# Memory's products moved behind the first group's queries, with x's rows and query weights loaded ahead of memory, and two row tiles begun with products of high parts

## The chip, the cores and the metric

The kernel runs on 1 core of one Trainium2 chip. The metric is device time in microseconds of one execution; the median of several runs is compared. The engines are TensorE (PE, matmuls, with its weight loads shown as PEld), VectorE (DVE), ScalarE (ACT), GpSimd (POOL) and SyncE (SP), which here only issues DMA transfers from its queue (SPq).

## The reference

An encoder trunk of two layers on 512 tokens of width 1024, in fp32. Each layer mixes tokens, then applies a gated feed-forward net, with RMS norms before and after each. What matters here is the start of the first layer, whose mixer is banded attention (12 query heads in 3 groups, 3 key and value heads) beside 4 heads of attention on a memory of 256 rows:

```python
mem_n = rms_norm(mem, mem_norm_g)
for i in range(DEPTH):
    h = rms_norm(x, g_mix_pre[i])
    proj = h @ w_in[i]                 # q | k | v | qm
    ...                                # kind 0: rotary on part of q and k, banded attention with a sink per head
    mkv = mem_n @ w_mem_kv[i]          # km | vm, 256 rows
    mo = memory_attention(qm, km, vm)
    o = jnp.concatenate([tok, mo], axis=-1) @ w_o[i]
    x = x + rms_norm(o, g_mix_post[i])
    h = rms_norm(x, g_ffn_pre[i])
    gu = h @ w_gate_up[i]
    f = (jax.nn.silu(gu[..., :D_FF]) * gu[..., D_FF:]) @ w_down[i]
    x = x + rms_norm(f, g_ffn_post[i])
```

## The kernel before

Precision: every fp32 operand is split into a high part (a rounded copy, fp32r) and a low part (the rest). A product is three matmuls (`mm3`, lines 276 to 278): high by high, high by the weights' low part (`wlo`), low by the weights' high part (`whi`). The high part is made by ScalarE (line 286, or 303 with a gain) or GpSimd (284, 301), the low part by VectorE (290, 304) or GpSimd (288). A unit's `side` says who: bit 2 puts the high part on GpSimd, bit 1 the low part.

Tiles: x is 4 row tiles of 128 tokens, its width 8 column tiles of 128 (`KD`). Transposed copies of x and of memory come from the host (`xT`, `memT`); `hT` and `mT` are their high and low parts with the norm's gain, while each row's own factor (`rs`, `rm`) is worked out from the plain rows (`row`, `mh`) and applied to the product. Weights come in units of two or four column tiles (`unit`): a raw buffer (`raw`, 3 of them) is loaded, then split into `whi` and `wlo` (4 buffers of each), mostly in two halves. All four units of the key and value weights (`wkv`) sit in those 4 buffers until tile 3 has used them; the next four units take them over in the order in which they were asked for.

Order on TensorE is written out by hand in `mixer`: `put(x, f)` lays a step at a coordinate x, and the steps are issued in the order of x. Head h of the attention begins at x = h; `kstep`, `q0step` and other entries of the table `PACE` give the length of a step. For layer 0 the start is, in this order: key and value products of the 4 row tiles (`kv_pieces`, each of 4 steps u of two column tiles, the first two tiles interleaved by the table `FIRST`), the transposes of their keys (`keys`), the products of the first group of queries (`q_pieces` with c = 0, 4 row tiles of 4 steps), the products of memory's keys and values (`mem_pieces`: 4 steps u for 2 row tiles m of memory), the first steps of query group 1, and the scores of head 0 (`score`, line 574). Memory's steps u = 0 and 1 stand right behind the last key product and ahead of the first query product; u = 2 and 3 lie between steps of the queries:

```python
xm = [max(xq + pc["m0off"], xk + 3.8 * k if l else xk)]
xm.append(xm[0] + pc["m0dur"])
```

The other engines' and SP's instructions are ordered by a planner with costs of its own, which follows the order in which the program asks for them where data and buffers allow; only the loads in `loads` are chained to go out one behind the other. `LATE` gives the coordinates of the work that is made on demand: forms of x's tiles 2 and 3, row factors `("r", t)`, memory's forms `("m", m)`, memory's plain rows (`"rows"`) and factors `("rm", m)`. Behind memory's last step `tok` copies `mT` (2 MB) to DRAM for layer 1, and the attention's output then takes its place. In `start`, 14 matmuls on zeros run while the first loads are on their way.

Of the kernel before, what the change touches and what calls it, by code (L numbers as in the profile page):

```python
# [16 lines left out]
P = 128  # L17
# [15 lines left out]
BIG = 1e37  # L33
NFILL = 3
URGENT = 150
FIRST = ((0, 0.25, 1, 1.5), (0.5, 0.75, 1.25, 1.75))
LATE = {2: 1.2, ("r", 0): 1.05, ("r", 1): 1.3, 3: 2.2, ("r", 2): 2.4, ("m", 0): 2.8, ("m", 1): 3.2, ("r", 3): 3.4,
        "rows": 2.5, ("rm", 0): 4.4, ("rm", 1): 4.5}
LOTS = ((0, 8), (8, 14), (14, 22))

PACE = [{'lag': 1.692, 'vlag': 0.479, 'jstep': 0.213, 'kstep': 0.375, 'klag': 0.742, 'qoff': [0.212, 0.126, 0.099], 'qlag': 1.02, 'late': 0.6, 'moff': -0.235, 'mdur': 0.562, 'mlag': 0.697, 'kw': [0, 0, 2, 0], 'mw': [2, 1, 1, 0], 'qw': [1, 0, 0, 1, 3, 3, 3, 3], 'hoff': 0, 'ow': [10.3, 10.8, 12.2, 13.2], 'ox': 11.4, 'od': 0.3, 'hstep': 0.872, 'hlag': 1.742, 'hjstep': 0.135, 'hvlag': 0.751, 'owm': [0, 0, 0, 0, 0, 0, 0, 0], 'q0step': 0.27, 'q0off': -0.032, 'q0lag': 0.919, 'm0off': -0.078, 'm0dur': 0.002, 'm0lead': 1.887, 'mlead': 1.201, 'qlead': 0.921, 'q0lead': 1.555, 'qstep': 1.002, 'tw': [0, 0, 0, 0, 0, 0, 0, 0], 'h2off': 0}, {'lag': 1.824, 'vlag': 0.535, 'jstep': 0.218, 'kstep': 0.777, 'klag': 1.715, 'qoff': [-0.027, -0.162, -0.027], 'qlag': 1.189, 'late': 2.15, 'moff': -0.088, 'mdur': 0.384, 'mlag': 1.205, 'kw': [0, 0, 0, 0], 'mw': [0, 0, 0, 0], 'qw': [0, 0, 0, 0, 0, 3, 1, 1], 'hoff': 0, 'ow': [10.2, 10.7, 12.2, 13.2], 'ox': 11.3, 'od': 0.3, 'hstep': 0.946, 'hlag': 1.847, 'hjstep': 0.295, 'hvlag': 0.568, 'owm': [0, 0, 0, 0, 0, 0, 0, 0], 'q0step': 0.718, 'q0off': -0.018, 'q0lag': 1.136, 'm0off': -1.059, 'm0dur': 0.171, 'm0lead': 2.465, 'mlead': 3.162, 'qlead': 1.895, 'q0lead': 1.42, 'qstep': 0.998, 'tw': [0, 0, 0, 0, 0, 0, 0, 0], 'h2off': 0.016}]

# [143 lines left out]
class Trunk:  # L186
# [195 lines left out]
    def mem_pieces(self, l, mk, put, x0, dx, lag, xw):  # L382

        nc = self.nc
        w, ps = {}, []
        for u in range(4):
            self.unit(self.a["wm"][l, u], self.side(l, "mw", u), put=put, x=xw[u], dst=w, key=u,
                      early=("wm", u) if l == 0 else None)

        def prod(u, m):  # L390
            if u == 0:
                ps.append(self.tagged("s"))
            for k in (2 * u, 2 * u + 1):
# [73 lines left out]
    def kv_pieces(self, l):  # L467
        nc = self.nc
        self.ka = self.core.tile([P, NG, S], F32R, name="ka", tag="ka")
        self.kb = self.core.tile([P, NG, S], F32R, name="kb", tag="kb")  # L470
        self.vs = self.core.tile([P, NT, NG, P], F32R, name="vs", tag="vs")
        w = self.wkv

        def prod(t, st, u):
            self.ready(t)
            if u == 0:
                st["ps"] = self.tagged("acc" if t < 2 else "s")
            ps = st["ps"]
            for k in (2 * u, 2 * u + 1):
                c = slice((k % 2) * 384, (k % 2) * 384 + 384)  # L480
                self.mm3(ps[:, :384], self.hslice(0, k, t * P, t * P + P), self.hslice(1, k, t * P, t * P + P),
                         w[u][0][:, c], w[u][1][:, c], k == 0, k == KD - 1)
            if u == 3:
                self.ready(("r", t))
                kv = ps[:, :384].rearrange("p (z h d) -> p z h d", z=2, d=HD)
                r = self.rs[:, t:t + 1]
                kx = self.core.tile([P, 4, HD], F32, tag="qx", name="kx", bufs=3)
                ins = nc.scalar.activation(kx[:, :NG], kv[:, 0], AF.Copy, scale=r).ins
                self.split_scaled(self.vs[:, t, :, :HD], self.vs[:, t, :, HD:], kv[:, 1], r)
                if l:  # L490
                    with self.tc.issue_after(ins):
                        z, ks = t // 2, slice(t % 2 * 4, t % 2 * 4 + 4)
                        nc.sync.dma_start(self.mT[:, z, ks].bitcast(F32), self.spill[:, z, ks])
                r = self.rope(l, kx, t, NG, 1)
                if l:
                    nc.vector.tensor_mul(kx[:, :NG], kx[:, :NG], r[:, :NG, None].to_broadcast([P, NG, HD]))
                st["k2"] = self.core.tile([P, 4, 3 * HD], F32R, tag="q2", name="k2", bufs=3)
                self.split(st["k2"][:, :NG, :HD], st["k2"][:, :NG, HD:P], kx[:, :NG])
                self.again(st["k2"][:, :NG])

        out = []
        for t in range(NT):
            st = {}
            out.append(([lambda t=t, st=st, u=u: prod(t, st, u) for u in range(4)],
                        lambda t=t, st=st: self.keys(st["k2"], self.ka, self.kb, t, NG)))
        return out

# [167 lines left out]
    def mixer(self, l, mkp, late, tokp):  # L675
# [59 lines left out]
        for z, key in enumerate(list(late)):  # L735
# [2 lines left out]
        lay(self.kv_pieces(l), xk, k, pc["klag"], lambda t: 0 if l else max(0, t - 1) / 4, None if l else FIRST)  # L738
        lay(self.q_pieces(l, 0, qT, put, xq + pc["q0off"], pc["q0lead"]), xq + pc["q0off"], pc["q0step"], pc["q0lag"],
            lambda t: t / 4)  # L740
        xm = [max(xq + pc["m0off"], xk + 3.8 * k if l else xk)]
        xm.append(xm[0] + pc["m0dur"])
        xm.append(max(xm[1] + pc["m0dur"], pc["moff"] - 1))
        xm.append(xm[2] + pc["mdur"])
# [405 lines left out]
    def start(self, mkp):  # L1150
# [3 lines left out]
        with ExitStack() as st:  # L1154
# [49 lines left out]
        def row(t):  # L1204
            rows[t] = [self.core.tile([P, 512], F32, tag=z, name="row", bufs=4) for z in ("th", "tl")]
            for z in range(2):
                queued(rows[t][z], a["x"][0, t * P:(t + 1) * P, 512 * z:512 * z + 512])

        def turn(t):
            xT.append(turned("xT"))  # L1210
            for z in range(2):
                queued(xT[t][:, 4 * z:4 * z + 4], a["xT"][t, z])

        def mem_turn(m):
            mT.append(turned("memT"))
# [145 lines left out]
```

## Time and profile before

| | us |
|---|---|
| median of 3 runs (1116.82 to 1117.99) | 1117.63 |
| profiled execution | 1118.46 |
| its span | 1116.6 |
| TensorE busy in the span | 1091.1 |
| VectorE busy | 842.1 |
| ScalarE busy | 660.1 |
| GpSimd busy | 196.7 |

The span is the time from the first to the last instruction of the profiled execution; its own time is 1.86 us longer. Busy times of engines overlap. A profile names an instruction by line, engine and operation, with what it writes and reads (`ps<-whi,mT`: a matmul into `ps` from those two tiles), and an idle time by what ended it. The granted clock is TensorE's, 1.00 at full speed. The start of the first layer up to the first score ends at 63.53 us.

### The profile page before, as it was taken

To read this page: it belongs to the slowest core of one execution; us is meant where nothing else is said; L and a number is where in the kernel's file an instruction comes from. 1 tells how busy PE (TensorE), PEld (TensorE's weight loads), DVE (VectorE), ACT (ScalarE), POOL (GpSimd) and SP (SyncE) were. 2 spreads that over 40 slices of the span, in tenths; PEclk is the share of its full clock that TensorE was granted. 3 is DMA by queue.
4 is the path that set the end of the run, shared out by engine and by line. 5 is a ranking of instruction groups with operands and counts; after the bars stand their busy time and mean duration, and the time that the engine had idled before them with its cause. 6 is when DMAs were issued, how large, how long until landed. Compare 5 with 4: busy or idle time off the path is not lost.

```text
span 1116.6 us, 19512 instructions
## 1 busy us (share of the span) xinstructions
PE 1091.1 (98%) x7438; PEld 1002.4 (90%) x7438; DVE 842.1 (75%) x1430; ACT 660.1 (59%) x1359; POOL 196.7 (18%) x340
## 2 busy tenths in 40 slices
PE   8899999999999999999999999999999999999997
PEld 7799988999889989998898888878999899899986
DVE  6778886899547867885787988767996478669855
ACT  6678984766445634653467788756664255345631
POOL 4574331202000000000343453312000000000001
PEclk9999999999999999999999999999999999999999
DMA  8621016443753372325443221145136223412253
GB/s 314 227 77 49 28 38 227 151 151 116 244 181 112 113 273 89 97 81 211 163 167 114 76 77 38 38 152 189 39 114 213 70 80 114 148 64 98 87 169 114
DMA packets 40557, 142.43 MB, mean 128 GB/s; under 512 B 4624, under 2 KB 5008, under 8 KB 40336
## 3 DMA queue, kind: packets, MB, share of 16 engines
q1 hardware_dynamic: 40176, 140.66, 36.5%
q8 instruction: 58, 0.95, 0.4%
q10 hardware_dynamic: 288, 0.53, 0.2%
q14 instruction: 35, 0.29, 0.1%
HBM read 122.30 MB, written 18.87 MB: 126 GB/s over the span
## 4 chain that ended last, share of the span: by engine, by line
PE 87%; DVE 6%; ACT 3%; POOL 2%; issue 1%; DMA 1%; DVEq 0%; POOLq 0%; ACTq 0%
PE ps L277 14%; PE ps L278 14%; PE ps L276 14%; PE ps L1034 12%; PE ps L1032 12%; PE ps L1033 12%; PE tp L635 3%; PE o L650 2%; PE o L649 2%; PE s L574 1%; PE s L575 1%; DVE tl L290 1%; DVE wlo L290 1%; DMA pair<-whi 1%; POOL r L310 1%
## 5 line engine op out<-in xcount | busy, mean ns | idle before, releaser
L286 ACT ACTIVATE whi<-raw 128x512 fp32r<-128x512 f32 (+3 forms) x204 | 168.7, 843 | 175.5 <-PE ps L1034 73.7
L290 DVE TENSOR_TENSOR wlo<-raw,whi 128x1024 fp32r<-128x1024 f32 (+3 forms) x199 | 192.5, 980 | 75.7 <-ACT whi L286 72.0
L1033 PE MATMUL ps<-sf,wlo 128*128 128x256 f32 x640 | 179.7, 281 | 0.0
L1032 PE MATMUL ps<-sf,whi 128*128 128x256 f32 x640 | 179.7, 281 | 0.0
L1034 PE MATMUL ps<-sf,whi 128*128 128x256 f32 x640 | 179.7, 281 | 0.0
L277 PE MATMUL ps<-wlo,f 128*128 128x512 f32 (+1 forms) x360 | 138.7, 385 | 0.1
L276 PE MATMUL ps<-whi,f 128*128 128x512 f32 (+1 forms) x360 | 138.7, 385 | 0.0
L278 PE MATMUL ps<-whi,f 128*128 128x512 f32 (+1 forms) x360 | 138.4, 385 | 0.0
L1034 PE MATMUL ps<-a,whi 128*128 128x256 f32 x480 | 134.4, 280 | 0.0
L1032 PE MATMUL ps<-a,whi 128*128 128x256 f32 x480 | 134.3, 280 | 0.0
L1033 PE MATMUL ps<-a,wlo 128*128 128x256 f32 x480 | 133.8, 279 | 0.0
L1033 PEld LDWEIGHTS ps<-sf,wlo 128*128 128x128 f32 x640 | 121.4, 190 | 0.5
L1032 PEld LDWEIGHTS ps<-sf,whi 128*128 128x128 f32 x640 | 121.1, 189 | 0.5
L1034 PEld LDWEIGHTS ps<-sf,whi 128*128 128x128 f32 x640 | 121.4, 190 | 0.0
L319 POOL TENSOR_SCALAR e<-sso 128x1 f32<-128x1 f32 x8 | 3.4, 421 | 564.3 <-ACT junk L314 564.2
L276 PE MATMUL ps<-whi,hT 128*128 128x256 f32 (+1 forms) x320 | 99.0, 309 | 1.3 <-ACT whi L286 1.3
L277 PE MATMUL ps<-wlo,hT 128*128 128x256 f32 (+1 forms) x320 | 94.7, 296 | 2.5 <-DVE wlo L290 2.5
L625 POOL TENSOR_SCALAR p<-p,rd 128x256 f32<-128x256 f32 (+2 forms) x128 | 76.8, 617 | 102.5 <-DVE rd L622 44.9
L278 PE MATMUL ps<-whi,hT 128*128 128x256 f32 (+1 forms) x320 | 94.2, 294 | 0.0
L1033 PEld LDWEIGHTS ps<-a,wlo 128*128 128x128 f32 x480 | 90.5, 188 | 0.2
L1032 PEld LDWEIGHTS ps<-a,whi 128*128 128x128 f32 x480 | 90.4, 188 | 0.2
L1034 PEld LDWEIGHTS ps<-a,whi 128*128 128x128 f32 x480 | 90.1, 188 | 0.0
(203 smaller groups left out, 2697.9 us busy)
## 6 DMA issues: line engine op xcount, KB each, us to landing
raw<-in_wgu_dram SPq DMA_DIRECT2D x48, 512.0 KB, 4.4
raw<-in_wd_dram SPq DMA_DIRECT2D x44, 512.0 KB, 4.4
rb<-in_wgu_dram SPq DMA_DIRECT2D x40, 512.0 KB, 3.6
raw<-in_wo_dram SPq DMA_DIRECT2D x17, 512.0 KB, 4.1
raw<-in_wq_dram SPq DMA_DIRECT2D x16, 512.0 KB, 5.1
xt<-x SPq DMA_DIRECT2D x12, 512.0 KB, 4.8
raw<-in_wm_dram SPq DMA_DIRECT2D x8, 512.0 KB, 4.0
x<-y SPq DMA_DIRECT2D x8, 512.0 KB, 2.9
```

The lines of the kernel that those rows point to most:

```text
L276: mm(out, lh, rh, start=first, stop=False)
L277: mm(out, lh, rl, start=False, stop=False)
L278: mm(out, ll, rh, start=False, stop=last)
L286: a = nc.scalar.activation(hi, src, AF.Copy)
L290: b = nc.vector.tensor_sub(lo, src, hi.bitcast(F32))
L625: self.pooled = nc.gpsimd.tensor_scalar(hd["p"][z][:, :n], hd["p"][z][:, :n], rd[:, z:z + 1], 1.0, op0=OP.mult, op1=OP.mult)
L635: nc.tensor.transpose(tp[:, z], hd["p"][i][:, jj * P:(jj + 1) * P], self.ident)
L649: nc.tensor.matmul(o[:, c0:c1], hd["v"](j), th, start=(j == 0), stop=False, skip_group_check=True)
L650: nc.tensor.matmul(o[:, c0:c1], hd["v"](j), tl, start=False, stop=last, skip_group_check=True)
L1032: mm(out, wh[:, s], rh, start=start and k == 0, stop=False, skip_group_check=True)
L1033: mm(out, wl[:, s], rh, start=False, stop=False, skip_group_check=True)
L1034: mm(out, wh[:, s], rl, start=False, stop=k == 3, skip_group_check=True)
```

## The change

Five edits go together. Memory's steps u = 0 and 1 move from ahead of the first query product to a place between the last two steps of the last row tile of query group 0; u = 2 and 3 follow at their old distance. The coordinates of memory's forms, rows and factors move accordingly. The queue of loads takes x's rows and both query units (`wq`, z = 0 and 1) ahead of memory; memory's second weight unit loses its place in the queue and is loaded by the ordinary path when a raw buffer is free. For row tiles 0 and 1 the first two steps are split: the high by high products of both steps come first (`which` 0), then the products with a low part (`which` 1). At the very start, the high parts of tile 0's column tiles 4 to 7 are made by GpSimd instead of ScalarE, and the second unit of `wkv` is split in two halves instead of in one piece. In the table `PACE`, the first entry of layer 0's `qw` goes from 1 to 0, so the first query unit's low part is made by VectorE instead of GpSimd.

```diff
-FIRST = ((0, 0.25, 1, 1.5), (0.5, 0.75, 1.25, 1.75))
-LATE = {2: 1.2, ("r", 0): 1.05, ("r", 1): 1.3, 3: 2.2, ("r", 2): 2.4, ("m", 0): 2.8, ("m", 1): 3.2, ("r", 3): 3.4,
-        "rows": 2.5, ("rm", 0): 4.4, ("rm", 1): 4.5}
+FIRST = ((0, 0.05, 0.1, 0.15, 1, 1.5), (0.5, 0.55, 0.6, 0.65, 1.25, 1.75))
+LATE = {2: 1.2, ("r", 0): 1.05, ("r", 1): 1.3, 3: 2.2, ("r", 2): 2.4, ("r", 3): 3.4, ("m", 0): 4.5, ("m", 1): 5,
+        "rows": 4, ("rm", 0): 6, ("rm", 1): 6.2}
...
             self.unit(self.a["wm"][l, u], self.side(l, "mw", u), put=put, x=xw[u], dst=w, key=u,
-                      early=("wm", u) if l == 0 else None)
+                      early=("wm", u) if l == u == 0 else None)
...
-        def prod(t, st, u):
+        def prod(t, st, u, which=None):
             self.ready(t)
-            if u == 0:
+            if u == 0 and which != 1:
                 st["ps"] = self.tagged("acc" if t < 2 else "s")
...
+                args = (ps[:, :384], self.hslice(0, k, t * P, t * P + P), self.hslice(1, k, t * P, t * P + P),
+                        w[u][0][:, c], w[u][1][:, c])
+                if which is None:
+                    self.mm3(*args, k == 0, k == KD - 1)
+                elif which == 0:
+                    nc.tensor.matmul(args[0], args[1], args[3], start=k == 0, stop=False)
+                else:
+                    nc.tensor.matmul(args[0], args[1], args[4], start=False, stop=False)
+                    nc.tensor.matmul(args[0], args[2], args[3], start=False, stop=False)
...
+            steps = [(0, 0), (1, 0), (0, 1), (1, 1), (2,), (3,)] if l == 0 and t < 2 else [(u,) for u in range(4)]
...
-        xm = [max(xq + pc["m0off"], xk + 3.8 * k if l else xk)]
+        xm = [max(xq + pc["m0off"], xk + 3.8 * k) if l else xq + 3.6 * pc["q0step"]]
...
-                                      gcol[:, 0, k:k + 1], 2 * (t > 0 and k % 2))
+                                      gcol[:, 0, k:k + 1], 2 * (k // 4 if t == 0 else k % 2))
...
-                self.wkv.append(self.unit(a["wkv"][0, u], side=self.side(0, "kw", u), raw=raw[u], parts=1 if u else 2))
+                self.wkv.append(self.unit(a["wkv"][0, u], side=self.side(0, "kw", u), raw=raw[u], parts=1 if u > 1 else 2))
...
         def loads():
             turn(2)
             row(0)
-            raw("wm", 0, a["wm"][0, 0])
             row(1)
             turn(3)
+            row(2)
+            for z in range(2):
+                raw("wq", z, a["wq"][0, 0, z])
+            row(3)
             mem_turn(0)
-            row(2)
-            raw("wm", 1, a["wm"][0, 1])
+            raw("wm", 0, a["wm"][0, 0])
             mem_turn(1)
-            row(3)
-            raw("wq", 0, a["wq"][0, 0, 0])
```

More of the change, by code (lines that the diff above doesn't have):

```diff
@@ L35 @@
 URGENT = 150
-FIRST = ((0, 0.25, 1, 1.5), (0.5, 0.75, 1.25, 1.75))
-LATE = {2: 1.2, ("r", 0): 1.05, ("r", 1): 1.3, 3: 2.2, ("r", 2): 2.4, ("m", 0): 2.8, ("m", 1): 3.2, ("r", 3): 3.4,
-        "rows": 2.5, ("rm", 0): 4.4, ("rm", 1): 4.5}
+FIRST = ((0, 0.05, 0.1, 0.15, 1, 1.5), (0.5, 0.55, 0.6, 0.65, 1.25, 1.75))
+LATE = {2: 1.2, ("r", 0): 1.05, ("r", 1): 1.3, 3: 2.2, ("r", 2): 2.4, ("r", 3): 3.4, ("m", 0): 4.5, ("m", 1): 5,
+        "rows": 4, ("rm", 0): 6, ("rm", 1): 6.2}
 LOTS = ((0, 8), (8, 14), (14, 22))
-PACE = [{'lag': 1.692, 'vlag': 0.479, 'jstep': 0.213, 'kstep': 0.375, 'klag': 0.742, 'qoff': [0.212, 0.126, 0.099], 'qlag': 1.02, 'late': 0.6, 'moff': -0.235, 'mdur': 0.562, 'mlag': 0.697, 'kw': [0, 0, 2, 0], 'mw': [2, 1, 1, 0], 'qw': [1, 0, 0, 1, 3, 3, 3, 3], 'hoff': 0, 'ow': [10.3, 10.8, 12.2, 13.2], 'ox': 11.4, 'od': 0.3, 'hstep': 0.872, 'hlag': 1.742, 'hjstep': 0.135, 'hvlag': 0.751, 'owm': [0, 0, 0, 0, 0, 0, 0, 0], 'q0step': 0.27, 'q0off': -0.032, 'q0lag': 0.919, 'm0off': -0.078, 'm0dur': 0.002, 'm0lead': 1.887, 'mlead': 1.201, 'qlead': 0.921, 'q0lead': 1.555, 'qstep': 1.002, 'tw': [0, 0, 0, 0, 0, 0, 0, 0], 'h2off': 0}, {'lag': 1.824, 'vlag': 0.535, 'jstep': 0.218, 'kstep': 0.777, 'klag': 1.715, 'qoff': [-0.027, -0.162, -0.027], 'qlag': 1.189, 'late': 2.15, 'moff': -0.088, 'mdur': 0.384, 'mlag': 1.205, 'kw': [0, 0, 0, 0], 'mw': [0, 0, 0, 0], 'qw': [0, 0, 0, 0, 0, 3, 1, 1], 'hoff': 0, 'ow': [10.2, 10.7, 12.2, 13.2], 'ox': 11.3, 'od': 0.3, 'hstep': 0.946, 'hlag': 1.847, 'hjstep': 0.295, 'hvlag': 0.568, 'owm': [0, 0, 0, 0, 0, 0, 0, 0], 'q0step': 0.718, 'q0off': -0.018, 'q0lag': 1.136, 'm0off': -1.059, 'm0dur': 0.171, 'm0lead': 2.465, 'mlead': 3.162, 'qlead': 1.895, 'q0lead': 1.42, 'qstep': 0.998, 'tw': [0, 0, 0, 0, 0, 0, 0, 0], 'h2off': 0.016}]
@@ new lines @@
+PACE = [{'lag': 1.692, 'vlag': 0.479, 'jstep': 0.213, 'kstep': 0.375, 'klag': 0.742, 'qoff': [0.212, 0.126, 0.099], 'qlag': 1.02, 'late': 0.6, 'moff': -0.235, 'mdur': 0.562, 'mlag': 0.697, 'kw': [0, 0, 2, 0], 'mw': [2, 1, 1, 0], 'qw': [0, 0, 0, 1, 3, 3, 3, 3], 'hoff': 0, 'ow': [10.3, 10.8, 12.2, 13.2], 'ox': 11.4, 'od': 0.3, 'hstep': 0.872, 'hlag': 1.742, 'hjstep': 0.135, 'hvlag': 0.751, 'owm': [0, 0, 0, 0, 0, 0, 0, 0], 'q0step': 0.27, 'q0off': -0.032, 'q0lag': 0.919, 'm0off': -0.078, 'm0dur': 0.002, 'm0lead': 1.887, 'mlead': 1.201, 'qlead': 0.921, 'q0lead': 1.555, 'qstep': 1.002, 'tw': [0, 0, 0, 0, 0, 0, 0, 0], 'h2off': 0}, {'lag': 1.824, 'vlag': 0.535, 'jstep': 0.218, 'kstep': 0.777, 'klag': 1.715, 'qoff': [-0.027, -0.162, -0.027], 'qlag': 1.189, 'late': 2.15, 'moff': -0.088, 'mdur': 0.384, 'mlag': 1.205, 'kw': [0, 0, 0, 0], 'mw': [0, 0, 0, 0], 'qw': [0, 0, 0, 0, 0, 3, 1, 1], 'hoff': 0, 'ow': [10.2, 10.7, 12.2, 13.2], 'ox': 11.3, 'od': 0.3, 'hstep': 0.946, 'hlag': 1.847, 'hjstep': 0.295, 'hvlag': 0.568, 'owm': [0, 0, 0, 0, 0, 0, 0, 0], 'q0step': 0.718, 'q0off': -0.018, 'q0lag': 1.136, 'm0off': -1.059, 'm0dur': 0.171, 'm0lead': 2.465, 'mlead': 3.162, 'qlead': 1.895, 'q0lead': 1.42, 'qstep': 0.998, 'tw': [0, 0, 0, 0, 0, 0, 0, 0], 'h2off': 0.016}]
@@ L480, in prod @@
                 c = slice((k % 2) * 384, (k % 2) * 384 + 384)
-                self.mm3(ps[:, :384], self.hslice(0, k, t * P, t * P + P), self.hslice(1, k, t * P, t * P + P),
-                         w[u][0][:, c], w[u][1][:, c], k == 0, k == KD - 1)
+                args = (ps[:, :384], self.hslice(0, k, t * P, t * P + P), self.hslice(1, k, t * P, t * P + P),
[7 more added lines that the diff above has]
+                    nc.tensor.matmul(args[0], args[2], args[3], start=False, stop=False)
             if u == 3:
@@ L503, in kv_pieces @@
             st = {}
-            out.append(([lambda t=t, st=st, u=u: prod(t, st, u) for u in range(4)],
+            steps = [(0, 0), (1, 0), (0, 1), (1, 1), (2,), (3,)] if l == 0 and t < 2 else [(u,) for u in range(4)]
+            out.append(([lambda t=t, st=st, z=z: prod(t, st, *z) for z in steps],
                         lambda t=t, st=st: self.keys(st["k2"], self.ka, self.kb, t, NG)))
```

## The prediction

> **What bounds the kernel now.** First the page's head, then TensorE's waits over the whole run (engine, line, what it waited for: us in total, times, longest).
>
> ```profile
> span 1116.6 us, 19512 instructions
> PE 1091.1 (98%) x7438; PEld 1002.4 (90%) x7438; DVE 842.1 (75%) x1430; ACT 660.1 (59%) x1359; POOL 196.7 (18%) x340
> PE 87%; DVE 6%; ACT 3%; POOL 2%; issue 1%; DMA 1%; DVEq 0%; POOLq 0%; ACTq 0%
> ...
> PE ps L276 <- ACT mT L303: 4.5, 1, 4.5
> ```
>
> TensorE is busy 98% of the span, and the chain that ended last lies on it for 87%. So time comes out only where TensorE idles or runs slowly, and what is saved early is kept by the busy rest. The longest wait of the run, 4.5 us, is one matmul's wait for `mT`, memory's high and low parts. The stretches of 3.4 us around the start show the rest (columns: engines' busy time with instructions, granted clock, DMA share, GB/s).
>
> ```profile
> 7.62:11.04 3.42, 1.83 (x9) 1.27 (x8) 3.42 (x10) 3.12 (x8) 3.15 (x5) 1.00 0.98 368
> 11.04:14.42 3.38, 3.38 (x12) 3.38 (x12) 3.38 (x7) 1.34 (x5) 2.39 (x6) 0.50 0.74 268
> ...
> 28.07:31.49 3.42, 1.59 (x8) 0.91 (x6) 2.45 (x9) 1.27 (x4) 2.06 (x7) 1.00 0.70 230
> 31.49:34.90 3.41, 0.73 (x2) 0.30 (x2) 3.41 (x6) 1.96 (x7) 3.35 (x5) 1.00 0.59 233
> 34.90:38.31 3.41, 2.78 (x7) 2.20 (x8) 3.19 (x12) 2.30 (x8) 2.39 (x7) 0.51 0.45 154
> ```
>
> Twice TensorE starves (1.83 us busy of 3.42; later 0.73 of 3.41), and each time the next stretch runs at a clock of 0.50 or 0.51. A starved stretch is paid twice: in idle time, then in matmuls of double length. But 1.59 of 3.42 was followed by 1.00, so no threshold can be read off.
>
> Both places in the order of time (start, duration, engine, line, operation; idle before it):
>
> ```profile
> 6.63 0.44 PE L276 MATMUL ps<-whi,hT 128*128 128x384 f32 x1 [0.77 <-ACT whi L286]
> ...
> 10.40 0.45 PE L277 MATMUL ps<-wlo,hT 128*128 128x384 f32 x1 [1.01 <-DVE wlo L290]
> ...
> 19.04 0.33 PE L278 MATMUL ps<-whi,hT 128*128 128x384 f32 x1
> 19.21 0.33 PE L276 MATMUL ps<-whi,hT 128*128 128x384 f32 x1
> ...
> 28.10 0.39 PE L276 MATMUL ps<-whi,mT 128*128 128x512 f32 x1
> 28.33 0.40 PE L277 MATMUL ps<-wlo,mT 128*128 128x512 f32 x1
> ...
> 34.14 0.50 PE L276 MATMUL ps<-whi,mT 128*128 128x512 f32 x1 [4.48 <-ACT mT L303]
> 35.53 0.80 PE L278 MATMUL ps<-whi,mT 128*128 128x512 f32 x1 [0.65 <-DVE mT L304]
> 36.13 0.63 PE L276 MATMUL ps<-whi,mT 128*128 128x512 f32 x1
> 36.55 0.63 PE L277 MATMUL ps<-wlo,mT 128*128 128x512 f32 x1
> ...
> 46.11 0.28 PE L277 MATMUL ps<-wlo,hT 128*128 128x256 f32 x1
> 46.23 0.28 PE L278 MATMUL ps<-whi,hT 128*128 128x256 f32 x1
> ...
> 63.53 0.28 PE L574 MATMUL s<-ka,qT 128*128 128x256 f32 x1
> ```
>
> **Part 1: two row tiles begin with high parts.** The key and value products of tiles 0 and 1 are 48 matmuls, from 6.63 to 19.21. At full clock one follows the other by 0.17 us (19.04 to 19.21; 0.173 as a mean over a longer stretch), so 48 need 8.3 us; 12.6 - 8.3 = 4.3 us are lost. Of these, ten or so in the stretch at clock 0.50 cost about 0.16 us more each, 1.6 us; the other 2.7 us are gaps behind weights' high and low parts (1.01 us at 10.40 the longest) and what each restart costs. The change adds no matmul: of the first two steps of a tile the high-by-high products come first, the eight products with a low part after them, so four matmuls can run while VectorE still makes low parts. The first weights' second unit is also split in halves (one ACTIVATE and one TENSOR_TENSOR become two each, a fixed cost of some 0.1 us a piece: 768 columns took 0.946 us and 384 took 0.555, below), and tile 0's high parts of columns 4 to 7 move from ACT to POOL: four operations.
>
> ```profile
> L304 DVE SCALAR_TENSOR_TENSOR hT<-xT,cst,hT 128x128 fp32r<-128x128 f32 x4 | 1.2, 352 | 4.1 <-ACT hT L303 4.1
> L290 DVE TENSOR_TENSOR wlo<-raw,whi 128x384 fp32r<-128x384 f32 x2 | 1.0, 555 | 0.2 <-ACT whi L286 0.2
> L304 DVE SCALAR_TENSOR_TENSOR hT<-xT,cst,hT 128x128 fp32r<-128x128 f32 x5 | 2.4, 543 | 0.0
> L290 DVE TENSOR_TENSOR wlo<-raw,whi 128x768 fp32r<-128x768 f32 x1 | 0.9, 946 | 0.0
> 14.63 2.18 DVE L304 SCALAR_TENSOR_TENSOR hT<-xT,cst,hT 128x128 fp32r<-128x128 f32 x8
> 7.89 2.62 POOL L301 TENSOR_SCALAR hT<-xT,cst 128x128 fp32r<-128x128 f32 x4 [7.07 <-DMA xT<-in_xT_dram]
> ```
>
> VectorE is the floor. It is busy without a break from 6.6 until these two tiles and all four weight units are done at 14.63 (the row there is tile 2's), and the change gives it no less to do. The last product cannot end before about 15.2, so the gain is at most 19.2 - 15.2 = 4.0 us. Below it is a loss: VectorE's operation took 352 ns with POOL idle (4 to 7.5 us) and 543 ns with POOL busy (11 to 13), so four more on POOL slow about eight of VectorE's by up to 0.19 us, 1.5 us. Where the high-first order wins nothing, about a third of that could come out, -0.5. The Trainium skill ("SBUF — State Buffer", Who interferes with whom) says that a VectorE operation with two inputs in SBUF and a GpSimd operation that reads SBUF exclude each other. The two rows agree in direction; by that rule VectorE would lose up to POOL's whole 2.62 us for four such operations, the floor would rise from 15.2 to 17.8, the gain would be held to 1.4 and the sum below would be 1112.0. I take the whole clock loss, 1.6 us, as gone, for with products from about 8 us on the stretch is fuller; half of the gaps, 1.3; less 0.6 for tile 3's parts and the rows' factors, which must now be ready 3 us sooner. Gain **2.3 us**, ends -0.5 and 4.0.
>
> **Part 2: memory's products move.** Before, the first four steps of memory (u 0 and 1, both row tiles) stood at 28.10, right behind the last key product. Now they and one more stand behind q's third step of its last row tile. What goes: 4.48 and 0.65 us of idling, and the matmuls at half clock from 35.53: they follow each other by 0.42 us where 0.23 is usual (28.10 to 28.33), about seven of them, 1.5 us with the slow restart. **6.6 us**.
>
> What hides memory's parts then? Between the last key product and memory's first stand 15 of q's 16 steps at six matmuls 0.12 us apart (46.11 to 46.23; 0.72 us a step, 10.8) and three pairs of key transposes (about 0.45 each, 1.4): 12.2 us. VectorE, ACT and POOL have this to do before the first score, in what was 35.5 us and would be 28.9:
>
> ```profile
> 28.10:63.60 35.50, 30.36 (x204) 27.07 (x204) 23.71 (x56) 22.26 (x55) 21.04 (x35) 0.95 0.57 206
> 63.60:150.00 86.40, 83.03 (x651) 79.76 (x651) 76.05 (x227) 76.12 (x221) 39.52 (x63) 1.00 0.14 45
> L304 DVE SCALAR_TENSOR_TENSOR mT<-memT,cst,mT 128x128 fp32r<-128x128 f32 x16 | 6.4, 452 | 0.0
> L288 POOL TENSOR_TENSOR wlo<-raw,whi 128x512 fp32r<-128x512 f32 x10 | 13.1, 1334 | 10.8 <-ACT whi L286 10.8
> L286 ACT ACTIVATE whi<-raw 128x512 fp32r<-128x512 f32 x14 | 8.1, 624 | 0.2 <-PE ps L278 0.2
> ```
>
> That is 82%, 77% and 73%: it fits, though VectorE has little left. `mT` takes 6.4 us of VectorE within those 12.2. One query unit moves its low parts from POOL to VectorE: two of 1.3 us off POOL, two of about 0.65 on VectorE (a little over the 0.555 for 384 columns). Two weight units are tight: memory's units 2 and 3 take the buffers of q's two units, and the last of these is free only behind q's last step, some 2.8 us before memory's last step (0.3 of transposes, 1.4, 0.72, 0.3), against about 2.6 for two highs (0.62 each, ACT) and lows. I take 1.0 us for VectorE and 0.5 for that unit; ends 0 and 3.0.
>
> **Part 3: the queue.** SP's order changes; the sum of bytes does not (memory's second unit goes, the second query unit comes).
>
> ```profile
> 9.37 1.38 SPq L1202 DMA_DIRECT2D row<-in_x_dram  x2
> 13.83 0.33 SPq L1202 DMA_DIRECT2D memT<-in_memT_dram  x1
> ...
> 19.14 0.33 SPq L1202 DMA_DIRECT2D raw<-in_wq_dram  x1
> ...
> raw<-in_wq_dram SPq DMA_DIRECT2D x1, 512.0 KB, 8.0
> 43.00 0.43 SPq L705 DMA_DIRECT2D smem<-mT  x1
> ...
> smem<-mT SPq DMA_DIRECT2D x1, 2048.0 KB, 10.4
> raw<-in_wq_dram SPq DMA_DIRECT2D x1, 512.0 KB, 5.2
> ```
>
> All blocks are 512 KB, so a block takes the landing of the one that stood in its place. Memory's second transposed block is last, where wq was: 19.14 + 8.0 = 27.1, 11 us ahead of its product. q's first unit takes the place at 13.83 and lands by about 21; its buffer comes free with tile 3's first step, near 23, later than that. So loading costs nothing; without that cover each place further back would cost about 1.3 us (the eight places from 9.37 to 19.14 lie 1.2 us apart). Moved behind it: memory's rows (needed only where memory's keys are scaled, behind its last step), a weight unit loaded by the ordinary path, and the 2 MB copy of `mT` to DRAM, priced below.
>
> **Sum.** 1118.46 (this execution, 0.83 above the median 1117.63) - 2.3 - 6.6 + 1.5 = **1111.1**. With every unknown at its good end 1107.9.
>
> **Rivals.** (a) The half clock stays at the start: the gaps shrink but the stretch still falls below what the gate wants. For it: 54% busy was followed by 0.50. Against: 47% by 1.00. It gives back 1.6: 1112.7. Beside it stands a rule of the Trainium skill ("TensorE: Matmul & The Clock Gate", Part 1): throttled is the default, an activity window of about 3.4 us decides, and it runs free of the kernel's start, so which products are slow depends on its phase. The trace agrees with the length, 3.4 us.
> (b) VectorE becomes the bound between 25 and 54 us: memory's steps or q's transposes wait some 4.5 us instead of 1.5. For it: 82% in order. Against: it was idle for 11.8 of those 35.5 us. 1114.3, three more than the forecast's waits.
> (c) It doesn't do what it says: memory's forms are late again at the new place, with idle and slow clock, and only part 1 is left: 1116.2. Needs `mT` 5 us later than 38; only a planner's order that puts it behind everything gives that.
> (d) Slower: the copy of `mT` (10.4 us) now becomes ready while group 1's query weights are still to be loaded. If it goes out at about 41 ahead of both units, the second lands at 41 + 10.4 + 5.2 + 3.5 = 60.1, and its low part (0.62 + 1.33) is ready at 62.0, where its product stands 1.8 us before the first score, at 52.8: 9.2 us of waiting and 1.6 of slow clock, 1121.9. It turns slower (over 1119.9) once those parts are ready after 60. Against: before, that load went out at 49.45 while the copy ran from 43.00 to 53.4, and took 5.2.
>
> **How the numbers follow.** Runs spread over 0.1%; 0.2% (2.2 us) is what can be told from no change. Forecast 0.51, (a) 0.10, (b) 0.17, (c) 0.12, (d) 0.10. Faster: forecast, (a) and (b), 0.78. Same: (c), 0.12. Slower: 0.10. The range goes from 1107.3 (good ends, and the median's 0.8 in part) to 1117.5, leaving out (d) and part of (c).
>
> **What the profile will show.** Right: no wait of TensorE for `mT`; 0.98 and more clock in every stretch from 11 to 42 us; tile 2's first product near 16.9; first score at 54 to 57 where it was at 63.53. Part 1 wrong: tile 2's first product at 18 or later, or a stretch at 0.50. Part 2 wrong: waits of TensorE for `wlo`, `whi`, or `mT` between 25 and 55 of over 3 us together. The prediction fails as a whole if the rest of the layer, where VectorE and ACT are busy 76 of 86 us, gives the lead back: TensorE's idle time behind the first score would grow above the 3.4 us of that row (86.40 - 83.03).

## The result, and the profile after

The changed kernel took 1112.22 us (median of 4 runs, 1110.48 to 1113.25) against 1117.81 us for the kernel before in the same measurement (1116.82 to 1118.67): a ratio of 0.9949, interval 0.9931 to 0.9966. The profiled execution took 1110.48 us, the lowest of the four, where the one before took 1118.46. The two profiles therefore differ by 8.0 us and the medians by 5.6; experiments 9 to 12 are about the other 2.4.

The head of the page after, then TensorE's longest waits over the whole run (what it waited for: us in total, times, longest):

```profile
span 1108.7 us, 19514 instructions
PE 1089.4 (98%) x7438; PEld 1000.2 (90%) x7438; DVE 840.7 (76%) x1433; ACT 658.5 (59%) x1356; POOL 196.2 (18%) x342
```

```profile
PE ps L277 <- DVE wlo L290: 2.9, 3, 1.5
PE tp L643 <- DVE tl L290: 2.5, 7, 0.7
...
PE tp L429 <- DVE kmb L430: 1.2, 1, 1.2
```

The wait for `mT` is gone. A new one heads the list: a weight's low part, once for 1.5 us. The stretches that were shown of before, now of after (engines' busy time with instructions, granted clock, DMA share, GB/s):

```profile
7.62:11.04 3.42, 3.42 (x17) 2.83 (x17) 3.42 (x8) 2.22 (x6) 3.42 (x7) 1.00 0.92 353
11.04:14.42 3.38, 1.63 (x8) 1.09 (x8) 3.38 (x9) 1.97 (x8) 1.94 (x6) 1.00 0.73 265
...
34.90:38.31 3.41, 3.41 (x33) 3.41 (x32) 3.41 (x11) 2.59 (x7) 2.09 (x3) 1.00 0.57 167
```

At 34.90 TensorE is full at full clock, where it ran at 0.51 before. At the start the picture is not what was forecast: the stretch before 11.04 is now full (17 matmuls, 9 before), but the next one holds only 1.63 us of work (8 matmuls; 12 before, at clock 0.50). The starved stretch has moved by one place, and the lead at its end is four matmuls. TensorE in the order of time (start, duration, operation, idle before it):

```profile
12.35 0.33 PE L276 MATMUL ps<-whi,hT 128*128 128x384 f32 x1
...
14.22 0.45 PE L277 MATMUL ps<-wlo,hT 128*128 128x384 f32 x1 [1.54 <-DVE wlo L290]
...
18.34 0.33 PE L276 MATMUL ps<-whi,hT 128*128 128x384 f32 x1
...
27.22 0.28 PE L276 MATMUL ps<-whi,hT 128*128 128x256 f32 x1
...
39.62 0.40 PE L276 MATMUL ps<-whi,mT 128*128 128x512 f32 x1
...
56.05 0.28 PE L582 MATMUL s<-ka,qT 128*128 128x256 f32 x1
```

These rows place the gain. Tile 2's first product is 0.9 us sooner (18.34; 19.21 before), and the end of the key products still is (27.22; 28.10). From there to the first score it takes 28.83 us instead of 35.43, 6.6 less; the score is 7.5 sooner. From the first score to the end of the span it takes 1052.65 instead of 1053.07 us. All but 0.4 us of the 7.9 between the spans was gained before 56 us.

### The profile page after: what moved, and what is told of

Its sections match the earlier page's. It is cut to its first block, busy times and chain, and to the rows that moved or that the text cites. A ratio compares the mean times of both kernels' runs of the same rounds, so it can differ in the third digit from the quotient of the medians.

```text
span 1108.7 us, 19514 instructions
## 1 busy us (share of the span) xinstructions
PE 1089.4 (98%) x7438; PEld 1000.2 (90%) x7438; DVE 840.7 (76%) x1433; ACT 658.5 (59%) x1356; POOL 196.2 (18%) x342
## 4 chain that ended last, share of the span: by engine, by line
PE 88%; DVE 5%; ACT 2%; POOL 2%; issue 1%; DMA 1%; DVEq 0%; POOLq 0%; SPq 0%; ACTq 0%
PE ps L277 14%; PE ps L276 14%; PE ps L278 14%; PE ps L1042 12%; PE ps L1041 12%; PE ps L1040 12%; PE tp L643 3%; PE o L658 2%; PE o L657 2%; PE s L582 1%; PE s L583 1%; DVE tl L290 1%; POOL r L310 1%; DVE tok L666 1%; ACT junk L314 1%
## 5 line engine op out<-in xcount | busy, mean ns | idle before, releaser
L286 ACT ACTIVATE whi<-raw 128x1024 fp32r<-128x1024 f32 (+3 forms) x205 | 168.5, 839 | 176.9 <-PE ps L1042 73.5
L290 DVE TENSOR_TENSOR wlo<-raw,whi 128x1024 fp32r<-128x1024 f32 (+3 forms) x202 | 190.9, 960 | 73.5 <-ACT whi L286 71.5
L276 PE MATMUL ps<-whi,hT 128*128 128x256 f32 (+1 forms) x312 | 95.2, 305 | 0.0
L277 PE MATMUL ps<-wlo,hT 128*128 128x256 f32 (+1 forms) x312 | 91.1, 292 | 2.9 <-DVE wlo L290 2.9
L278 PE MATMUL ps<-whi,hT 128*128 128x256 f32 (+1 forms) x312 | 90.9, 291 | 0.0
```

Source lines behind the costliest of these rows:

```text
L276: mm(out, lh, rh, start=first, stop=False)
L277: mm(out, lh, rl, start=False, stop=False)
L278: mm(out, ll, rh, start=False, stop=last)
L286: a = nc.scalar.activation(hi, src, AF.Copy)
L290: b = nc.vector.tensor_sub(lo, src, hi.bitcast(F32))
```

## Experiments

### 1 and 2: each half alone

The first kernel is the changed one with the start's order and shares of before:

```diff
-FIRST = ((0, 0.05, 0.1, 0.15, 1, 1.5), (0.5, 0.55, 0.6, 0.65, 1.25, 1.75))
+FIRST = ((0, 0.25, 1, 1.5), (0.5, 0.75, 1.25, 1.75))
-            steps = [(0, 0), (1, 0), (0, 1), (1, 1), (2,), (3,)] if l == 0 and t < 2 else [(u,) for u in range(4)]
+            steps = [(u,) for u in range(4)]
-                                      gcol[:, 0, k:k + 1], 2 * (k // 4 if t == 0 else k % 2))
+                                      gcol[:, 0, k:k + 1], 2 * (t > 0 and k % 2))
-                ... parts=1 if u > 1 else 2))
+                ... parts=1 if u else 2))
```

> Only memory's steps and the queue of loads are changed; the start (order of high and low parts, split of the second unit, POOL's share of tile 0) is as before. Theory: the two parts are separate, memory's move is worth its 4.48 + 0.65 us of idling and 1.5 us of slow clock, so 1117.8 - 6.6 = 1111.2, no wait for mT, and the start as before (tile 2's first product at 19.2, a stretch at half clock there). With the start's edits worth 0.9 us (19.21 to 18.34 in the two profiles) it is at most 1113.1. Rival, the start's edits carry 2 us or more of the gain, as the prediction had it: 1114.3 or more.

Measured: 1112.63 us (1112.15 to 1113.39), ratio 0.9954, interval 0.9941 to 0.9966. In its profile the start is that of before, half clock included, and the first score stands at 58.14:

```profile
11.04:14.42 3.38, 3.38 (x12) 3.38 (x12) 3.38 (x7) 1.56 (x5) 3.13 (x6) 0.53 0.73 263
```

```profile
58.14 0.28 PE L582 MATMUL s<-ka,qT 128*128 128x256 f32 x1
```

Moving memory with its loads makes the gain of the medians by itself; the start's edits add 0.4 us to it, which this measurement can't tell from nothing. The forecast for this run, 1111.2, was missed by 1.4 us. From the key products' end (28.16) to the first score it takes 29.98 us, 1.15 more than in the changed kernel, and 0.82 us go to two waits for a low part of memory's weights, which the changed kernel's profile does not have:

```profile
46.96 0.50 PE L277 MATMUL ps<-wlo,mT 128*128 128x512 f32 x1 [0.54 <-POOL wlo L288]
48.20 0.50 PE L277 MATMUL ps<-wlo,mT 128*128 128x512 f32 x1 [0.28 <-POOL wlo L288]
```

The second kernel is the other half: the changed start, with the place, forms (`LATE`), loads and `qw` of memory as before (shown here against the changed kernel).

```diff
-        xm = [max(xq + pc["m0off"], xk + 3.8 * k) if l else xq + 3.6 * pc["q0step"]]
+        xm = [max(xq + pc["m0off"], xk + 3.8 * k if l else xk)]
... (LATE, loads(), early and the first entry of 'qw' as before)
```

> Only the start is changed; memory's steps and the queue stand as before. Theory: what the start wins, 0.9 us, is lost again at memory's first steps, because the wait there ends with mT's parts, which come from loads and from VectorE, ACT and POOL and not from TensorE; the wait grows from 4.5 to about 5.4 and the time is 1117.0 to 1117.9. Rival, the wait moves along with TensorE: it stays 4.5 and the time falls by 0.9 or more, to 1116.9 or less; by the prediction's size of part 1 to 1115.5.

Measured: 1118.08 us (1116.81 to 1119.57), ratio 1.0000, interval 0.9991 to 1.0009. Nothing is gained, as the theory had it, but not by the route it named:

```profile
27.61 0.44 PE L278 MATMUL ps<-whi,hT 128*128 128x384 f32 x1 [1.30 <-DVE hT L304]
...
33.37 0.50 PE L276 MATMUL ps<-whi,mT 128*128 128x512 f32 x1 [2.87 <-ACT mT L303]
```

The lead was gone before memory: the low parts of x's tile 3 came late (1.30 us at 27.61), as VectorE made the low part of a memory weight unit ahead of them (1.84 us from 25.15). Memory's wait did not grow, it is 2.87 us where 4.48 had been, and it ended 0.8 us sooner (33.37 against 34.14). That was lost again behind it: the granted clock was 0.50 from 33.8 to 40.6 us, two stretches of 3.4 us, where the kernel before had one, and the first query product stood at 41.41 against 40.62. How many of the eleven runs had the second such stretch is not shown.

### 3: the loads as before, memory late

What was priced at nothing was the loading. This kernel keeps all of the change but takes `loads` and `early` back:

```diff
         def loads():
             turn(2)
             row(0)
+            raw("wm", 0, a["wm"][0, 0])
             row(1)
             turn(3)
-            row(2)
-            for z in range(2):
-                raw("wq", z, a["wq"][0, 0, z])
-            row(3)
             mem_turn(0)
-            raw("wm", 0, a["wm"][0, 0])
+            row(2)
+            raw("wm", 1, a["wm"][0, 1])
             mem_turn(1)
+            row(3)
+            raw("wq", 0, a["wq"][0, 0, 0])
```

> The changed kernel with the queue of loads as before: memory's two weight units and its blocks ahead, q's first unit last, q's second unit by the ordinary path. Theory: the new order of products needs the new queue. q's first unit lands at about 27.1, just where its product stands, and the second can be asked for only when a raw buffer is free and goes out behind the 2 MB copy of mT, at about 33 us, where its product stands near 30: a wait of 9 to 14 us and a stretch at half clock, 1122 to 1128. Rival, as the prediction put it, loading costs nothing because the blocks trade places: 1112.2 to 1114.

Measured: 1128.40 us (1127.58 to 1129.88), ratio 1.0094, interval 1.0076 to 1.0112: 16 us behind the changed kernel and 10 behind the one before. Its queue, TensorE and one of its stretches:

```profile
33.26 0.33 SPq L713 DMA_DIRECT2D smem<-mT  x1
...
35.73 0.33 SPq L230 DMA_DIRECT2D raw<-in_wq_dram  x1
```

```profile
34.42 0.58 PE L276 MATMUL ps<-whi,hT 128*128 128x256 f32 x1 [7.00 <-ACT whi L286]
...
42.49 0.58 PE L276 MATMUL ps<-whi,hT 128*128 128x256 f32 x1 [3.78 <-ACT whi L286]
```

```profile
31.49:34.90 3.41, 0.48 (x1) 0.29 (x1) 3.00 (x12) 2.35 (x7) 1.43 (x5) 0.50 0.36 154
```

The query products now stand where memory's stood: 10.8 us of waiting for two units' high parts, and half clock from 30.1 to 50.6 us. The two waits have different causes. The second unit goes out behind the copy of `mT`, and ScalarE waited 3.14 us for its landing at 41.8. That is the mechanism of rival (d), met one query group sooner, and the changed queue keeps it away. The first unit had landed at 27.2 already (issued at 18.78, 8.4 us to landing), but ScalarE made its high part only at 33.74, behind row sums of x and behind an operation that waited for a row's factor; why the planner put it there with this queue is not shown. "Loading costs nothing" is true of the two edits together only.

### 4 and 5: what held the start

The order of VectorE in the changed kernel (start, duration, operation, number):

```profile
8.55 4.75 DVE L304 SCALAR_TENSOR_TENSOR hT<-xT,cst,hT 128x128 fp32r<-128x128 f32 x12
13.22 1.82 DVE L290 TENSOR_TENSOR wlo<-raw,whi 128x768 fp32r<-128x768 f32 x2
```

The low part for which TensorE waits at 14.22 stands behind twelve low parts of x: four of tile 0, and all eight of tile 1, of which half are not yet needed. The next kernel asks for tile 1 in two halves, with weight unit 2 between them. It adds and removes no instruction.

```diff
-                if u < 2:
-                    parts(*((0, (1,)), (1,))[u])
+                if u < 3:
+                    parts(*((0, (1,)), (1, (0,)), (1, (1,)))[u])
```

> The changed kernel with the third weight unit split ahead of the last four columns of tile 1 instead of behind all eight (VectorE made twelve low parts of x in a row, 8.55 to 13.3 us, before that unit's low part). Theory: VectorE's order, not its sum, holds tile 0's third step; its second product goes from 14.22 to about 12.7, tile 2's first from 18.34 to about 17.2, and with less idling the half clock is rarer: 1109.4 to 1111.1. Rival, VectorE's sum is the floor as the prediction had it: the wait moves to the fourth unit, tile 2 begins no sooner, 1112.2.

Measured: 1107.30 us (1106.99 to 1107.86), ratio 0.9905, interval 0.9889 to 0.9920. It beats both kernels, and is the fastest version found. VectorE, then TensorE:

```profile
8.37 3.47 DVE L304 SCALAR_TENSOR_TENSOR hT<-xT,cst,hT 128x128 fp32r<-128x128 f32 x8
11.76 0.94 DVE L290 TENSOR_TENSOR wlo<-raw,whi 128x768 fp32r<-128x768 f32 x1
12.63 1.27 DVE L304 SCALAR_TENSOR_TENSOR hT<-xT,cst,hT 128x128 fp32r<-128x128 f32 x4
```

```profile
12.76 0.45 PE L277 MATMUL ps<-wlo,hT 128*128 128x384 f32 x1 [0.25 <-DVE wlo L290]
...
16.89 0.33 PE L276 MATMUL ps<-whi,hT 128*128 128x384 f32 x1
...
25.79 0.28 PE L276 MATMUL ps<-whi,hT 128*128 128x256 f32 x1
...
54.39 0.28 PE L582 MATMUL s<-ka,qT 128*128 128x256 f32 x1
```

The wait is 0.25 instead of 1.54 us, and tile 2's first product stands at 16.89, the place forecast for the change itself. Of the 4.9 us between the medians the profiles show 2.6: 1.7 before the first score (54.39 against 56.05) and 0.9 behind it. The other 2.3 are that the changed kernel's profiled run lies 1.7 us below its median, and this one's 0.6 above. All four runs here have a mean granted clock of 0.999, while the changed kernel's four go from 0.995 to 0.999.

Then the same kernel with the plain order of products (`FIRST` and `steps` of before, as in experiment 1):

> The kernel with the third unit split sooner (1107.3 us), without the order that puts products of high parts first: tiles 0 and 1 take each column's three products together again. Theory: VectorE's order sets the pace, and the high-first order is worth little: at most 0.5 us, 1107.3 to 1107.8, tile 2's first product within 0.4 us of where it was. Rival, as the prediction had it: high-first fills the gaps behind the first low parts, and without it the 1.3 us of gaps and at times 1.6 of half clock come back: 1108.6 to 1110.

Measured: 1107.68 us (1107.07 to 1108.75), ratio 0.9902, interval 0.9886 to 0.9917. A tile that begins with high parts is worth 0.4 us here by the medians, which is not told from nothing. In the plain order TensorE waits sooner and longer:

```profile
10.87 0.45 PE L278 MATMUL ps<-whi,hT 128*128 128x384 f32 x1 [1.20 <-DVE hT L304]
```

Yet tile 2's first product stands at 17.02, only 0.13 later than with high parts first: what the order wins before 11 us it waits for again, for VectorE makes the same parts in the same order and within 0.1 us of the same times.

### 6: less work for GpSimd at the start

The kernel of experiment 4, with tile 0's high parts of columns 4 to 7 back on ScalarE:

```diff
-                                      gcol[:, 0, k:k + 1], 2 * (k // 4 if t == 0 else k % 2))
+                                      gcol[:, 0, k:k + 1], 2 * (t > 0 and k % 2))
```

> The kernel with the third unit split sooner (1107.3 us) and, of the changed kernel's edits, one undone: tile 0's high parts of columns 4 to 7 made by ScalarE again, not by GpSimd. By the prediction, four operations fewer on GpSimd free VectorE of up to 1.5 us: tile 2's first product comes sooner and the time is 1106.0 to 1107.0. Rival, ScalarE is the scarcer: its four operations of 0.31 us stand ahead of the second unit's high part and of tile 1's, the products with high parts wait for them, 1107.9 to 1108.6.

Measured: 1108.48 us (1108.18 to 1110.37), ratio 0.9917, interval 0.9903 to 0.9931, which overlaps that of experiment 4. In the profile the key products ended slightly sooner (25.54 against 25.79) and the first score stood later (55.42 against 54.39). What lies between are waits at memory's products for low parts of its weights, which experiment 4 does not have:

```profile
44.24 0.50 PE L277 MATMUL ps<-wlo,mT 128*128 128x512 f32 x1 [0.46 <-POOL wlo L288]
45.49 0.50 PE L277 MATMUL ps<-wlo,mT 128*128 128x512 f32 x1 [0.27 <-POOL wlo L288]
```

Who makes these four parts is not shown to matter for the start, though the waits behind it differ.

### 7 and 8: memory's wait filled with work

What share of the 6.6 us is idle time, and what share the clock behind it? In the kernel before, 18 more matmuls into a bank that nobody reads were put where TensorE waits for `mT`:

```diff
+            if l == 0 and u == 0 and m == 1:
+                idle = self.tagged("pv")
+                for _ in range(18):
+                    nc.tensor.matmul(idle, self.mT[:, 0, 0, :P], w[0][0][:, :512], start=True, stop=True)
```

> The kernel before with 18 extra matmuls (of 512 columns, into a bank that nobody reads) in memory's wait, between its first step for row tile 0 and that for row tile 1. They end no wait, they only keep TensorE busy. Theory: of the 6.6 us that memory's move saved, 1.5 were the half clock behind the idling: this kernel runs the matmuls from 35.5 us on at full clock and takes 1117.9 - 1.5 = 1116.4, with the first score near 62. Rival, the half clock is not due to the idling or hides nothing: 1117.9 or more.

Measured: 1122.91 us (1121.30 to 1123.71), ratio 1.0040, interval 1.0026 to 1.0053. The test failed: the added matmuls themselves waited 5.33 us for their bank, from which VectorE had yet to copy transposed keys:

```profile
33.81 5.87 PE L396 MATMUL ps<-whi,mT 128*128 128x512 f32 x18 [5.33 <-DVE kb L434]
```

So again with the bank of the products, `self.tagged("acc")`:

> As the filled wait before, but the 18 extra matmuls write a bank that is free by then (they had to wait 5.33 us for the one that the keys' transposes use, and so stood behind the wait instead of in it). Theory: they run in memory's wait, end about when it ends, and the matmuls behind it are at full clock: 1.5 us less than before, 1116.4, first score near 62. Rival, the idling alone is what costs: 1117.9.

Measured: 1118.33 us (1116.42 to 1120.54), ratio 0.9998, interval 0.9987 to 1.0008.

```profile
28.32 4.24 PE L396 MATMUL ps<-whi,mT 128*128 128x512 f32 x18
33.02 0.50 PE L276 MATMUL ps<-whi,mT 128*128 128x512 f32 x1 [0.46 <-ACT mT L303]
```

```profile
34.90:38.31 3.41, 3.41 (x17) 2.67 (x15) 2.49 (x11) 2.29 (x8) 2.06 (x6) 1.00 0.28 112
```

This time the wait was filled and the clock stayed at 1.00. From memory's waiting product to the first query product it took 5.16 us instead of 6.48, so the clock share, some 1.3 us, is there. But from the key products' end to the first score it took 34.92 us (26.95 to 61.87) where it had been 35.43: some 0.8 us of it was lost again between the first query product and the score, half of that in a wait for a low part (0.40 us at 38.86) that the kernel before does not have, and the whole time did not fall. So the clock's share alone is not gained here; the 6.6 us come with the moved order, not with a filled gap.

### 9 to 12: where the run-to-run spread comes from

The gap before 14.22 was filled in the changed kernel with 8 matmuls ahead of tile 0's third step:

```diff
+            if l == 0 and t == 0 and u == 2:
+                idle = self.tagged("pv")
+                for _ in range(8):
+                    nc.tensor.matmul(idle[:, :384], self.hslice(0, 0, 0, P), w[0][0][:, :384], start=True, stop=True)
```

> The changed kernel with eight extra matmuls (into a bank that nobody reads) ahead of tile 0's third step, where TensorE waited 1.54 us for wlo. Theory: the four runs of the changed kernel (1110.5 to 1113.3, mean clock 0.999 to 0.995) differ by whether a stretch of 3.4 us around that gap is followed by half clock, 1.6 us each; with the gap filled no run gets one, so all lie near 1110.5 with mean clock 0.999, a median 1.7 us under the changed kernel's 1112.2. Rival, the spread comes from elsewhere: median 1112.2 and the same spread; if the fillers delay real products, up to 1.4 us more.

Measured: 1109.94 us, ratio 0.9928, interval 0.9916 to 0.9941, and five runs within 0.4 us (1109.61 to 1110.02) where the changed kernel's four lie within 2.8. The spread is gone, yet the first score stood 1.2 us later (57.26) and the rest was shorter (1050.9 us), so the fill is not shown to be the whole cause. Two more profiles of the changed kernel, unaltered:

> The changed kernel once more, unaltered, for a second profile. Theory: when the time is near 1112.2 or over, the profile shows a stretch of 3.4 us at half clock between 11 and 18 us, which the first profile (1110.48) does not have, and the first score comes some 1.6 us later than 56.05; when it is near 1110.5, none. Rival, a run of 1112 has full clock there and is slower elsewhere.

> The changed kernel once more, unaltered, in three rounds. Theory: its times follow the mean clock in steps of one stretch at half clock (0.0015 of mean clock, 1.7 us): about 1110.5 at 0.998 or 0.999, 1112.2 at 0.997, 1113 and over at 0.995. If a run with 0.997 is the one that is profiled, the half clock stands right behind the 1.5 us wait at 14 us. Rival, times do not go with the clock.

The first took 1110.61 us and had no stretch at half clock, though the starved stretch at 11.04 was there again. The second took 1111.99 (four runs: 1110.92 to 1112.63, ratio 0.9936, interval 0.9915 to 0.9957), and the half clock was in another place:

```profile
60.40:63.81 3.41, 0.81 (x9) 0.67 (x7) 3.40 (x8) 2.66 (x7) 3.41 (x5) 0.97 0.55 154
63.81:67.22 3.41, 3.33 (x18) 3.36 (x19) 2.58 (x11) 1.96 (x6) 1.87 (x4) 0.53 0.49 150
```

Ahead of it a wait for memory's keys had grown from 1.20 to 2.68 us. What came ahead of it, in the rows of this profile and then of the changed kernel's first:

```profile
57.54 1.29 POOL L288 TENSOR_TENSOR wlo<-raw,whi 128x512 fp32r<-128x512 f32 x1
57.61 1.30 DVE L440 TENSOR_TENSOR rt<-qx,cst 128x64 f32<-128x64 f32 x1
63.89 0.34 PE L429 MATMUL tp<-identr,k 128*128 128x128 f32 x1 [2.68 <-DVE kmb L430]
```

```profile
57.63 0.23 DVE L440 TENSOR_TENSOR rt<-qx,cst 128x64 f32<-128x64 f32 x1
57.67 1.34 POOL L288 TENSOR_TENSOR wlo<-raw,whi 128x512 fp32r<-128x512 f32 x1
62.45 0.25 PE L429 MATMUL tp<-identr,k 128*128 128x128 f32 x1 [1.20 <-DVE kmb L430]
```

A VectorE operation of 0.23 us took 1.30 when GpSimd's began 0.07 us ahead of it, and ended with it (58.91 and 58.83). Where VectorE began first, by 0.04 us, neither lost more than 0.05. A race of less than 0.1 us decides over 1.1 of the 1.5 us here, and the clock drops behind the longer wait; most of the rest is a later VectorE operation (L290, 1.27 instead of 0.81 us), again beside one of GpSimd. The Trainium skill ("SBUF — State Buffer", Who interferes with whom) says that a VectorE operation with two inputs in SBUF contends with a GpSimd operation that reads SBUF, and that whoever issues first keeps the shared ports while the other blocks; the first pair of rows agrees; in the second GpSimd's operation took 0.05 us more (1.34 against 1.29) where VectorE had 0.19 us left to run, which is too little to tell. If the race were all, taking that low part off GpSimd should help (layer 0's `qw`, fifth entry):

```diff
-'qw': [0, 0, 0, 1, 3, 3, 3, 3]
+'qw': [0, 0, 0, 1, 2, 3, 3, 3]
```

> The changed kernel with one unit's low parts (the first of query group 2, two TENSOR_TENSORs) made by VectorE instead of GpSimd; in the second profile of the changed kernel (1111.99) GpSimd began them 0.07 us before a VectorE operation instead of 0.04 us behind it, that operation took 1.30 instead of 0.23 us, the copy of memory's keys came 1.4 us later and a stretch at half clock followed. Theory: this race makes the changed kernel's spread (1110.5 to 1113.3); with GpSimd's pair gone the VectorE operation is short every time, the wait for memory's keys is at most 1.3 us, no run is above 1111.6 and the median is 1110.3 to 1111.3. Rival: VectorE's two further operations of 0.65 us stand in front of memory's evictions and of the first scores, and cost what they win: 1112 or more.

Measured: 1112.09 us (1111.94 to 1113.40), ratio 0.9949, interval 0.9935 to 0.9962: no gain. VectorE had the work itself, and a score waited 1.79 us for it. Behind that wait its profiled run (1113.40) has half clock again, from 62.1 to 65.5 us, so the race is not the only way to it (last two rows). The run shows the other place too, behind the unaltered start (first two):

```profile
11.04:14.42 3.38, 1.64 (x7) 1.17 (x8) 3.38 (x9) 1.68 (x6) 2.33 (x6) 0.98 0.75 272
14.42:17.83 3.41, 3.41 (x12) 3.41 (x12) 2.64 (x9) 1.68 (x6) 2.20 (x6) 0.52 1.06 403
...
60.40:63.81 3.41, 2.22 (x13) 2.25 (x14) 3.41 (x10) 1.00 (x3) 3.41 (x4) 0.74 0.50 154
63.81:67.22 3.41, 3.41 (x27) 3.41 (x27) 2.90 (x10) 3.13 (x11) 0.19 (x1) 0.76 0.51 159
```

The same gap (1.64 and 1.63 us busy) was followed by 0.52 here and by 1.00 in the three profiles of the changed kernel; here the key products ended at 28.70 instead of 27.22, 1.5 us. So there are two places, each worth about 1.5 us, at which a run is served full clock or half. That fits a spread of 2.8 us. The mean granted clock, which is on record for every run, mostly goes with the time: 0.999, 0.997, 0.997 and 0.995 for 1110.48, 1112.16, 1112.28 and 1113.25 us in the first measurement; one later run breaks the order (0.999 for 1111.55). At which of the two places an unprofiled run lost its clock is not recorded.

## Why the prediction was right, and where its terms were off

**Part 2** was right in its mechanism: 6.6 us were forecast and 6.6 gained up to the first score (35.43 to 28.83), and all stretches from 14.4 to 42 us ran at 1.00. The term that was mis-sized is "1.0 us for VectorE and 0.5 for that unit". TensorE has no wait of 0.15 us or more between 14.3 and 56 us, so it was 0 of 1.5. That is in part luck: in experiments 1, 6 and 9, with memory moved in the same way, low parts of memory's weights did come late, by 0.82, 0.73 and 0.62 us in all, and the way from the key products to the score took 29.8 to 30.0 us instead of 28.83. The tight unit was a real risk; the 1.0 us for VectorE shows in no run with the changed queue. VectorE's work did fit:

```profile
27.20:56.05 28.85, 28.85 (x204) 26.36 (x203) 20.59 (x53) 19.12 (x51) 18.35 (x29) 1.00 0.63 227
56.05:142.45 86.40, 82.35 (x644) 78.76 (x643) 76.22 (x228) 75.74 (x219) 41.32 (x64) 1.00 0.16 53
```

It is busy 20.59 of 28.85 us, 71%, not the 82% of the sum; some of the work of the old 35.5 us now lies ahead of it (19.5 us before 27.2, where 18.5 lay before 28.1). A smaller bill came later: idle time in the 86.40 us behind the first score went from 3.4 to 4.05 us (86.40 - 82.35). The sign named for failure was met by 0.7 us, while the whole from the first score to the end still came out 0.4 shorter, so the lead was not given back.

**Part 1** is the step that failed: 2.3 us were forecast and 0.9 came (18.34, not 16.9; the prediction had called 18 or later wrong). Its floor was VectorE's sum of work, done by 14.63. The sum was nearly right (done by 15.04, 0.4 later, where GpSimd's four further operations had been priced at up to 1.5 us), and the order was not looked at: the low part of unit 2 stood behind twelve others (1.54 us), and the starved stretch moved by one place rather than going away. "The whole clock loss, 1.6 us, as gone" held in three profiles of the changed kernel by the outcome of the run, not by a fuller stretch. The 2.3 us are real, though: with VectorE's order altered, the key products ended 2.3 sooner than before (25.79 against 28.10). The high-first order, which the prediction made the carrier of this part, is not what brings it (experiment 5).

**Part 3** held, with its condition: the copy of `mT` went out at 46.24 us, behind the query units of group 1, and rival (d) did not come. Experiment 3 shows the price when the queue is not changed, 16 us.

**The rivals.** (a), the half clock at the start, is in none of the three profiles of the changed kernel (one has it at 63.6 us); it came in the kernel of experiment 12, where it cost 1.5 us against the 1.6 priced. (b) and (c) did not come: no wait for VectorE from 25 to 54 us, and none for memory's forms. By its own terms (b) is 1111.1 + 3.0 = 1114.1, not 1114.3. And the second half of a split costs 0.16 us by the prediction's own rows (2 x 0.555 - 0.946), not some 0.1.

**The sum**: in the profiles 0.9 + 6.6 + 0.4 = 7.9 of 8.0 us gained, against 7.4 forecast. That the total came so near is luck: part 1 was 1.4 us too high and the waits of part 2 were 1.5 too high, and the two errors cancel. In the medians it is 5.6, since the changed kernel's profiled run is its fastest and the kernel before's was slower than its median. Not settled is why the part behind the first score differs between these kernels by up to 2 us (1050.9 to 1053.07) with the same work in it.

## What to carry to other kernels

Move a step away from a wait together with the queue of its loads: the same move was worth 5.6 us with the new order of loads and cost 10 with the old one. Where an engine is busy without a break, its sum gives the floor, but its order decides who waits; one low part behind twelve others cost 1.5 us, and moving it up brought more than all the other edits to the start. Gains do not add: the start's edits were worth 0 alone, 0.4 with memory moved, and a further 4.9 with VectorE in the right order.

## What the hardware showed unexpectedly

The same idling has two outcomes. A stretch of 3.4 us with 1.63 or 1.64 us of work was followed by a clock of 1.00 in the three profiles of the changed kernel and by 0.52 in that of experiment 12; the start of the kernel before (1.83 or 1.84 busy) gave 0.50 in its profile and 0.53 in that of experiment 1, and 1.00 in those of experiments 7 and 8. Where half clock came, it cost about 1.5 us. The Trainium skill ("TensorE: Matmul & The Clock Gate", Part 1) says that the window in which activity is judged runs free of the kernel's start. The runs agree, and their clock records show where the windows lie.

Within a run all changes of the granted clock lie whole multiples of 3.41 us apart (before: 11.05, 14.47, 34.95 and 38.36; experiment 12: 14.27, 17.69, 62.06 and 65.47), and the offset differs from run to run. So 11.04 to 14.42 is not the window of every run. In the kernel before and in experiment 1 one window (from 7.64 and from 7.43) held 1.82 us of work, in experiment 12 one (from 10.86) held 1.66, and each time half clock followed. In the runs with full clock the windows fell otherwise over the same gaps: two of them shared it (2.11 and 2.97 us busy in the changed kernel's first profile, 2.40 and 2.70 in experiment 7, 2.22 and 2.88 in experiment 8), or one held 1.88 us (from 12.3 and 12.4, the changed kernel's other two). The outcome at the start thus goes with how the windows happen to cut the gap. Busy time alone still does not decide: in the kernel before, 1.54 us in the window from 28.12 was followed by 1.00.
